# Channel mean and variance in a hybrid decoder layer: fp32 products replaced by high and low parts in the matmul's type

## The chip, the cores and the metric

The kernel runs on one core of a Trainium2 chip. The metric is device microseconds of one execution; lower is better. Engines: PE (TensorE, matmuls), DVE (VectorE), ACT (ScalarE), POOL (GpSimd) and SP (which issues most DMAs). Each takes its instructions from its own queue, in order.

## The reference

One decoder layer over 1024 tokens and 16 meta tokens, width 1024. What matters here is the convolution branch:

```python
c = c_val * jax.nn.sigmoid(c_gate)              # 512 channels
c = causal_dwconv(c, conv_dw, conv_dw_b)        # 31 taps
c = jax.nn.silu(layer_norm(c, conv_ln_g, conv_ln_b))
y_conv = c @ w_conv_proj

def layer_norm(x, g, b):
    xf = x.astype(jnp.float32)
    mu = xf.mean(-1, keepdims=True)
    var = jnp.square(xf - mu).mean(-1, keepdims=True)
    return ((xf - mu) * lax.rsqrt(var + LN_EPS) * g + b).astype(x.dtype)
```

The LayerNorm runs over the 512 channels of each token.

## The kernel before

Activations lie with channels on the partitions and tokens along the free axis. The convolution's result is four chunks of 128 channels, `acc[0..3]`, of U = 1026 tokens each. A sum over channels is therefore a sum over four tiles and then over 128 partitions; the second is a matmul with `ones`, a 128x128 tile that holds 1/512, which leaves the mean in every partition. `ones` and what it multiplies are fp32 (F); the kernel's other large products run in fp32r (R), each factor split into a high and a low part (`split`: a cast on ACT writes the high part, a subtraction on DVE the low one).

The tokens are handled in three groups, UG: 258, 384 and 384 columns. In order:

- `csum` (line 947) is the sum of the four chunks: two additions on POOL, one on DVE (L951).
- The means (L956): one matmul per group, `ones` times `csum`, into the PSUM tiles `ps_m`. Their rank is RK_EVAC, high; `after(ins, gate_mm[10][0])` keeps them behind the first part of gate tile 10.
- `cln_centre` (L998) subtracts the means on DVE, four operations per group.
- `cln_var` squares the four chunks on ACT (L1004, L1007), adds the squares on DVE (L1008) in temporaries of five buffers, and takes the sum over partitions with a matmul (L1010).
- `cln_rstd` takes a reciprocal root on ACT (L1015) and refines it by a Newton step on DVE (L1016 to L1019). `cln_scale` multiplies on DVE (L1026) and applies SiLU on ACT (L1027), all SiLUs behind the last root. `cln_split` writes the high and low parts of the result into `OC` (L1033, L1034) for the projection; `o_split` does the same for the attention's output.

The DVE operations from `cln_centre` to `o_split` are pinned: each is put behind the one before it (`pin`). The order of the calls is: centre of the groups 0, 1, 2; variance of 0, 1, 2; rstd 0, rstd 1, scale 0, rstd 2, scale 1, scale 2; then the splits.

At the same time PE multiplies the gate tiles (`gate_tile`, `z_group`): a tile is four groups of about 256 tokens, each 24 matmuls in fp32r (L339, L342, L343), into one of three accumulators with the tag "mm". ACT evacuates each with a Tanh (L735) and sends it to DRAM from its own queue (L128). The weights of each tile come by DMA and are split by ACT (L301) and DVE (L304). Behind the gate tiles the projections (`ps_p`) begin, which read `OA` and `OC`.

The order within a queue is fixed when the program is built: a planner takes the instruction of the best rank among those that it expects to be ready. Ranks that matter here: RK_SPLIT 500, RK_EVAC 600, RK_CLN 38000, RK_Z 40000; lower goes first. `after` adds an order between two instructions on one engine.

`ones` is made three times: at the start (it feeds the warm-up matmuls, L572), before the attention for the means, and after it for the variances.

Of the kernel before, what the change touches and what calls it, by code (L numbers as in the profile page):

```python
# [23 lines left out]
F = mybir.dt.float32  # L24
R = mybir.dt.float32r
AF = mybir.ActivationFunctionType
OP = mybir.AluOpType
AX = mybir.AxisListType

P = 128  # L30
# [6 lines left out]
U = T - U0  # L37
# [3 lines left out]
CW = 512  # L41
# [71 lines left out]
def tile_hybrid_layer(  # L113
# [3 lines left out]
    nc = tc.nc  # L117
    PSUM = bass.MemoryType.PSUM

    def dram(ap, offset, dims):  # L120
        return bass.AP(tensor=ap.tensor, offset=ap.offset + offset, ap=[list(d) for d in dims])

    def load(o, i):
        return nc.sync.dma_start(out=o, in_=i)
# [5 lines left out]
    def f32(ap):  # L130
        return ap.bitcast(F)

    def after(ins, first):

        tc.add_manual_dep(ins.ins, first.ins.name, mybir.DependencyInfo(
            mybir.DependencyClass.NoSync, mybir.DependencyReason.SCHED_ONLY), reason="order of work")

    @contextmanager
    def rank(p):

        saved = tc.cur_priority
        tc.cur_priority = p
        yield
        tc.cur_priority = saved
# [35 lines left out]
    start = ExitStack()  # L180
    sp = start.enter_context(tc.tile_pool(name="start", bufs=1, side="right", reuse_waits="tile"))
# [35 lines left out]
    cff, ident = (coll[:, a - n_right:b - n_right] for a, b in COLS[2:-1])  # L217
# [17 lines left out]
    b1col = lambda k: colA[:, 66 + k:67 + k]  # L235
    ffw = lambda t, c: cff[:, t * 44 + c:t * 44 + c + 1]

    def ones_of(pool, behind=None):
        t = pool.tile([P, P], F, name="ones", tag="ones", bufs=1)
        ins = nc.vector.memset(t, 1.0 / CW)  # L240
        if behind is not None:
            after(ins, behind)
        return t

    ones = ones_of(sp)
    qb = const2.tile([P, 4], F, name="qb")
    half_ = constr.tile([P, 1], F, name="half")
    nc.vector.memset(half_, 0.5)
# [70 lines left out]
    def weights(shape, fill):  # L319
        fills[0] += 1  # L320
        n = fills[0]
        own = n == 3
        raw = OB[:, 0:D].rearrange("p (k c) -> p k c", k=KC) if own else wraw(shape)
        with rank({1: 14, 2: 13, 3: 16, 4: 23}.get(n, RK_SPLIT)):
            last_fill.append(fill(raw))
        hi, lo = chunks(sp.tile([P, W_LEN], R, name="w3") if own else wsp())
        if n <= 3:
            return hi, lo, raw
        with rank(RK_SPLIT):
            last_split.append(split(raw, hi, lo))  # L330
            if n == 7:
                after(last_split[-1], cin_done[-1])
        return hi, lo
# [349 lines left out]
    ap = att.enter_context(tc.tile_pool(name="att", bufs=1, side="right", reuse_waits="tile"))  # L683
# [16 lines left out]
    def conv_chunk(c):  # L700
        sig = {}

        def g_evac(g, a, b, ps):
            sig[g] = stage(b - a)

            nc.scalar.activation(sig[g], ps, AF.Tanh, bias=bcol(10 + c), scale=0.5)  # L706
            nc.scalar.activation(sig[g], sig[g], AF.Identity, bias=half_, scale=0.5)

        gate_last.append(z_tile(in_cols(10 + c), ZG, g_evac, wt_c1 if c == 1 else None))
        cin = cp.tile([P, 16 + T], F, name="cin", tag="cin")  # L710
        nc.vector.memset(cin[:, 0:16], 0.0)

        def v_evac2(g, a, b, ps):
            cin_done.append(nc.vector.scalar_tensor_tensor(cin[:, 16 + a:16 + b], ps, bcol(6 + c), sig[g],
                                                           OP.add, OP.mult))

        z_tile(in_cols(6 + c), ZG, v_evac2)

        def taps():
            with rank(RK_CONV + c * 100):  # L720
                for j in range(TAPS):
                    wc = cdw[:, j * CH + c:j * CH + c + 1]
                    if j == 0:
                        nc.vector.tensor_scalar(acc[c], cin[:, j:j + U], wc, cdwb(c), OP.mult, OP.add)
                    else:
                        nc.vector.scalar_tensor_tensor(acc[c], cin[:, j:j + U], wc, acc[c], OP.mult, OP.add)  # L726

        return taps

    def gate_tile(i):  # L730
        b2, m = divmod(i, KC)

        def gate_evac(g, a, b, ps):
            t = stage(b - a)
            nc.scalar.activation(t, ps, AF.Tanh, bias=bcol(14 + i), scale=0.5)  # L735
            store(sgd[b2, m, :, a - U0:b - U0], t)

        gate_mm[i] = z_tile(in_cols(14 + i), TG, gate_evac)

    tc.cur_priority = RK_QKV + 2000  # L740
    ins = load(vd, dram(v1d, 0, [[0, P], [J_LEN, NH], [1, J_LEN]]))
# [11 lines left out]
    tc.cur_priority = RK_QKV + 5000  # L753
    cin8 = cin_done[-1]
    ones = ones_of(cp, cin8)
    vmT = ap.tile([P, 64], F, name="vmT")
    for t in (f32(vm[64:]), f32(pmTs[0][64:]), f32(pmTs[1][64:]), vmT):
        after(nc.vector.memset(t, 0.0), cin8)
    for g in range(NKV):
# [3 lines left out]
        for lo in (0, 64):  # L763
            for o, i in ((Kx[g][lo:, :, 16:144], kr[lo:, 16:T].rearrange("p (n c) -> p n c", c=P)),
                         (Kx[g][lo:, :, 0:16], kr[lo:, 0:16].unsqueeze(1).to_broadcast([P - lo, NB, 16]))):
                if lo == 0:
                    ins = nc.vector.tensor_copy(o, i)
                else:
                    ins = nc.vector.tensor_tensor(o, i, f32(o), OP.subtract)
# [11 lines left out]
    for q4 in range(2):  # L781
# [5 lines left out]
        for g in range(NKV):  # L787
            hi, lo = (V[:, q4 * 4:q4 * 4 + 4, g, i] for i in range(2))
# [22 lines left out]
    for h in range(NH):  # L811
        g, r = divmod(h, 4)
        o = ps[:2, h * 16:(h + 1) * 16]
        ins = nc.tensor.matmul(o, q0[g][0][:, r, 0:2], Kx[g][:, 0, 0:16], start=True, stop=False)
# [66 lines left out]
    for i in range(NB):  # L881
# [5 lines left out]
        for g in range(NKV):  # L887
            qh, ql = load_q(g, i) if i else (t[:, :, 2:] for t in q0[g])
            s = ap.tile([P, 4, 272], F, name="s", tag="s", bufs=3)
# [50 lines left out]
    for o in order:  # L940
        if isinstance(o, str):
            conv_chunk(int(o[1]))()
        else:
            gate_tile(o)
        if o == "c3":

            csum = cp.tile([P, 16 + T], F, name="csum", tag="cin")[:, :U]
            with rank(RK_EVAC):
                nc.gpsimd.tensor_tensor(csum, acc[0], acc[1], OP.add)
                nc.gpsimd.tensor_tensor(csum, csum, acc[2], OP.add)  # L950
                nc.vector.tensor_tensor(csum, csum, acc[3], OP.add)  # L951
    means = {}
    for g, (a, b) in enumerate(UG):
        with rank(RK_EVAC):
            means[g] = pat.tile([P, 512], F, name="ps_m", tag="st"[g % 2], bufs=2)
            ins = nc.tensor.matmul(means[g][:, :b - a], ones, csum[:, a:b], start=True, stop=True)  # L956
            after(ins, gate_mm[10][0])
    att.close()
    qsp_stack.close()

# [7 lines left out]
    tmp_p = tmp_stack.enter_context(tc.tile_pool(name="tmp", bufs=1, side="right", reuse_waits="tile"))  # L968

    ones = ones_of(tmp_p)  # L970

    def temp(n):
        return tmp_p.tile([P, 384], F, name="t", tag="t", bufs=5)[:, :n]

    def at_group(t, o, k, hl, a, b):

        x = k + hl * 4
        o += x * ZN - UG[0][1] if a else 8 * ZN + x * BS[0]
        return t[:, o + a:o + b]

    def conv(c, hl, a, b):
        return at_group(OC, OC_CV, c, hl, a, b)
# [3 lines left out]
    def pin(ins):  # L986

        if pinned:
            after(ins, pinned[-1])
        pinned.append(ins)  # L990

    dve = nc.vector
    sums, rstd, roots, silus = {}, {}, [], []
# [6 lines left out]
    def cln_var(g):  # L1000
        a, b = UG[g]
        n = b - a
        s_ = temp(n)
        nc.scalar.activation(s_, acc[0][:, a:b], AF.Square)  # L1004
        for c in range(1, CH):
            q_ = temp(n)
            nc.scalar.activation(q_, acc[c][:, a:b], AF.Square)  # L1007
            pin(dve.tensor_tensor(s_, s_, q_, OP.add))  # L1008
        sums[g] = pat.tile([P, 512], F, name="ps_m", tag="st"[g % 2], bufs=2)
        nc.tensor.matmul(sums[g][:, :n], ones, s_, start=True, stop=True)  # L1010

    def cln_rstd(g):
        n = UG[g][1] - UG[g][0]
# [42 lines left out]
    for g in range(3):  # L1056
        cln_var(g)
# [74 lines left out]
    for m in range(KC):  # L1132
        hi, lo = weights([P, KC, P], lambda raw: load(raw, w_ab[m]))
# [382 lines left out]
    for c in range(FC):  # L1516
        V4, X, Z, Y = (pup.tile([P, 1024], F, name=n, tag=n) for n in ("pw", "px", "pz", "py"))
        passes = ((1,), (0,)) if c == 0 else ((0, 1),)
        for subs in passes:
            last = subs == passes[-1]  # L1520
            w_next = iter(range(7))
            a, b = SUB[subs[0]][0], SUB[subs[-1]][1]
# [21 lines left out]
            def tt(*x):  # L1544
                with rank(RK_CHAIN):
                    return nc.vector.tensor_tensor(*x)  # L1546
# [30 lines left out]
            ins = tt(c22[:, a:b], c22[:, a:b], u13[:, a:b], OP.add)  # L1577
# [259 lines left out]
```

## Time and profile before

| | us |
|---|---|
| median of 3 runs | 1264.42 (1263.83 to 1264.93) |
| profiled execution | 1265.13 |
| its span | 1263.3 |
| means on PE (L956) | 349.5 to 351.25 of the span |
| variance sums on PE (L1010) | 358.9 to 365 |
| SiLUs on ACT (L1027) | 370.5 to 379.5 |
| first projection matmuls | from about 416 |

In the lines of the profile a time in front is microseconds from the start of the span, the next number the duration. `x6` counts instructions; an fp32 matmul shows as two. What stands in square brackets is idle time of the engine just before, and what ended it. In the list of waits the numbers are the total in us, how often, and the longest.

### The profile page before, as it was taken

How to read it: one execution, taken by the hardware profiler on the slowest of the kernel's cores; microseconds unless marked ns; L12 is line 12 of the kernel's file. 1: busy time of each engine (PE TensorE's matmuls, PEld its weight loads, DVE VectorE, ACT ScalarE, POOL GpSimd, SP SyncE). 2: the span in 40 equal slices, each digit the busy share in tenths (PEclk: the TensorE clock that was granted, in tenths of full speed). 3: DMA queues.
4: the chain of work that ended last, by engine and by line, in shares of the span. 5: the costliest groups of instructions: out<-in, count | busy, mean ns of one | idle time of the engine just before them, and what ended most of it. 6: DMA issues, size and time to landing. Idle time of an engine off the chain costs nothing.

```text
span 1263.3 us, 23034 instructions
## 1 busy us (share of the span) xinstructions
PE 1250.0 (99%) x9186; PEld 1182.3 (94%) x9186; DVE 1073.3 (85%) x1854; ACT 591.5 (47%) x1095; POOL 8.1 (1%) x9
## 2 busy tenths in 40 slices
PE   8999999999999999999999999999999999999997
PEld 8999999999999999788899999999999998888886
DVE  8888999999978577448999999998989977996697
ACT  7533355555472233335655555554555544444330
POOL 0000000001000000000000000000000000000000
PEclk9999999999999999999999999999999999999999
DMA  7385633432428354222145545454454566998712
GB/s 259 99 273 132 188 97 97 113 90 81 133 84 227 108 171 125 84 85 82 67 155 197 197 171 215 161 209 135 160 204 162 195 227 249 393 362 315 269 64 84
DMA packets 98701, 212.19 MB, mean 168 GB/s; under 512 B 11411, under 2 KB 38611, under 8 KB 98338
## 3 DMA queue, kind: packets, MB, share of 16 engines
q1 hardware_dynamic: 84474, 199.64, 47.3%
q10 hardware_dynamic: 14120, 11.08, 2.8%
q8 instruction: 72, 1.18, 0.4%
q14 instruction: 35, 0.29, 0.1%
HBM read 150.29 MB, written 62.70 MB: 169 GB/s over the span
## 4 chain that ended last, share of the span: by engine, by line
PE 93%; DVE 3%; DMA 2%; ACT 1%; issue 1%; SPq 0%; DVEq 0%; ACTq 0%
PE px L1538 14%; PE py L1538 9%; PE ps_x L1683 9%; PE ps_z L339 8%; PE ps_z L342 8%; PE ps_z L343 8%; PE ps_z L1683 5%; PE pz L1538 5%; PE pw L1538 5%; PE ps_p L342 2%; PE ps_p L339 2%; PE ps_p L343 2%; PE ps_w L343 2%; PE ps_w L339 2%; PE ps_w L342 2%; PE ps_z L557 2%
## 5 line engine op out<-in xcount | busy, mean ns | idle before, releaser
L339 PE MATMUL ps_z<-RHO,w 128*128 128x256 f32 (+2 forms) x864 | 243.9, 282 | 0.2 <-ACT FA L735 0.2
L342 PE MATMUL ps_z<-RHO,w 128*128 128x256 f32 (+2 forms) x864 | 243.6, 282 | 0.0
L343 PE MATMUL ps_z<-RHC,w 128*128 128x256 f32 (+2 forms) x864 | 243.1, 281 | 0.0
L339 PEld LDWEIGHTS ps_z<-RHO,w 128*128 128x128 f32 x864 | 162.8, 188 | 1.8 <-ACT FA L706 0.7
L342 PEld LDWEIGHTS ps_z<-RHO,w 128*128 128x128 f32 x864 | 162.5, 188 | 1.0
L343 PEld LDWEIGHTS ps_z<-RHC,w 128*128 128x128 f32 x864 | 162.7, 188 | 0.5
L726 DVE SCALAR_TENSOR_TENSOR FA<-cin,cdw,FA 128x1026 f32<-128x1026 f32 x120 | 152.4, 1280 | 0.7
L1360 DVE TENSOR_TENSOR RHO<-wr,RHO 128x512 fp32r<-128x512 f32 x94 | 64.0, 689 | 8.3 <-ACT RHO L1359 8.2
L1359 ACT CAST RHO<-wr 128x512 fp32r<-128x512 f32 x94 | 56.7, 619 | 23.3 <-DVE wr L1377 11.9
L301 ACT CAST w<-wr 128x1024 fp32r<-128x1024 f32 x37 | 38.8, 1048 | 60.4 <-PE ps_z L343 42.4
L735 ACT ACTIVATE FA<-ps_z,colr 128x258 f32<-128x258 f32 (+1 forms) x64 | 30.2, 473 | 69.5 <-PE ps_z L343 58.2
L1377 DVE TENSOR_TENSOR wr<-wr 128x512 f32<-128x512 f32 x88 | 60.6, 689 | 0.1
L304 DVE TENSOR_TENSOR w<-wr,w 128x1024 fp32r<-128x1024 f32 x37 | 45.1, 1219 | 17.9 <-ACT w L301 17.8
L1550 ACT COPY FA<-px 128x514 f32<-128x514 f32 (+2 forms) x23 | 13.2, 572 | 75.4 <-PE px L1538 75.4
L1360 DVE TENSOR_TENSOR w<-wr,w 128x512 fp32r<-128x512 f32 x60 | 40.8, 688 | 4.8 <-ACT w L1359 4.7
L1538 PE MATMUL px<-OA,RHO 128*128 128x258 f32 x324 | 43.2, 282 | 0.0
L1465 ACT ACTIVATE FA<-OB,coll 128x512 f32<-128x512 f32 x44 | 35.9, 815 | 14.9 <-DVE OB L1546 14.9
L1359 ACT CAST w<-wr 128x512 fp32r<-128x512 f32 x60 | 36.3, 618 | 13.9 <-DMA wr<-in_w_up_dram 6.8
L1538 PE MATMUL px<-OC,RHO 128*128 128x256 f32 x324 | 41.5, 277 | 0.0
L1550 ACT COPY OB<-px 128x514 f32<-128x514 f32 (+2 forms) x46 | 26.2, 569 | 32.7 <-PE px L1538 32.5
L1538 PE MATMUL px<-RHC,RHO 128*128 128x258 f32 (+1 forms) x312 | 41.1, 281 | 0.3 <-ACT OB L1550 0.3
L1538 PEld LDWEIGHTS px<-OA,RHO 128*128 128x128 f32 x324 | 40.5, 189 | 0.2 <-ACT OB L1550 0.2
(442 smaller groups left out, 3298.8 us busy)
## 6 DMA issues: line engine op xcount, KB each, us to landing
wr<-in_w_up_dram SPq DMA_DIRECT2D x44, 512.0 KB, 3.6
wr<-in_w_z_dram SPq DMA_DIRECT2D x29, 512.0 KB, 3.8
OB<-in_w_down_dram SPq DMA_DIRECT2D x24, 512.0 KB, 5.0
fd<-FA SPq DMA_DIRECT2D x44, 256.0 KB, 2.0
FA<-sd SPq DMA_DIRECT2D x15, 512.0 KB, 8.7
qt<-qd SPq DMA_DIRECT2D x28, 256.0 KB, 4.2
OB<-td SPq DMA_DIRECT2D x14, 512.0 KB, 9.9
sgd<-FA ACTq DMA_DIRECT2D x48, 128.0 KB, 2.9
```

Of the source, the lines that this page charges most:

```text
L301: ins = nc.scalar.copy(hi, raw)
L304: return nc.vector.tensor_tensor(lo, raw, f32(hi), OP.subtract)
L339: ins = nc.tensor.matmul(ps, al, bh, start=i == 0, stop=False)
L342: nc.tensor.matmul(ps, ah, bh, start=False, stop=False)
L343: last = nc.tensor.matmul(ps, ah, bl, start=False, stop=i == n - 1)
L726: nc.vector.scalar_tensor_tensor(acc[c], cin[:, j:j + U], wc, acc[c], OP.mult, OP.add)
L1359: nc.scalar.copy(hi, src)
L1360: ins = nc.vector.tensor_tensor(lo, src, f32(hi), OP.subtract)
L1377: ins = nc.vector.tensor_tensor(*x)
L1538: ins = nc.tensor.matmul(o, x[:, ks], bmat(sub, q, hl, k), start=first and k + j == 0, stop=k == 3 and j == 2, skip_group_check=not first)
L1550: copied.append(nc.scalar.copy(*x))
L1683: nc.tensor.matmul(banks[i], l[:, ts], r[:, ws], start=first and a and x + k == 0, stop=z and x == len(ops) - 1 and k == 2, skip_group_che ...
```

## The change

The means and the variance sums are taken as two fp32r products each. The thing to be summed is split into a high part, which ACT copies into fp32r, and a low part, which DVE subtracts; both are multiplied by `ones` in fp32r and accumulated in the same PSUM tile. 1/512 is a power of two. The parts of `csum` (`ch`, `cl`) are put into the buffers of the attention's scores (tag "s", three of them); those of the sum of squares (`hi`, `lo`) into the place in `OC` that `cln_split` fills for chunk 0 of the same group. The two later `ones` are made by a tensor_scalar operation on the identity matrix, in place of a memset.

```diff
-    def ones_of(pool, behind=None):
-        t = pool.tile([P, P], F, name="ones", tag="ones", bufs=1)
-        ins = nc.vector.memset(t, 1.0 / CW)
+    def ones_of(pool, behind=None, dtype=R):
+        t = pool.tile([P, P], dtype, name="ones", tag="ones", bufs=1)
+        if dtype is F:
+            ins = nc.vector.memset(t, 1.0 / CW)
+        else:
+            ins = nc.vector.tensor_scalar(t, ident, 0.0, 1.0 / CW, OP.mult, OP.add)
...
-    ones = ones_of(sp)
+    ones = ones_of(sp, dtype=F)
...
                 nc.vector.tensor_tensor(csum, csum, acc[3], OP.add)
+                ch, cl = (ap.tile([P, 4 * 272], R, name=n, tag="s", bufs=3)[:, :U] for n in ("ch", "cl"))
+                nc.scalar.copy(ch, csum)
+                nc.vector.tensor_tensor(cl, csum, f32(ch), OP.subtract)
...
-            ins = nc.tensor.matmul(means[g][:, :b - a], ones, csum[:, a:b], start=True, stop=True)
+            ins = nc.tensor.matmul(means[g][:, :b - a], ones, ch[:, a:b], start=True, stop=False)
             after(ins, gate_mm[10][0])
+            nc.tensor.matmul(means[g][:, :b - a], ones, cl[:, a:b], start=False, stop=True)
...
             pin(dve.tensor_tensor(s_, s_, q_, OP.add))
+        hi, lo = (conv(0, hl, a, b) for hl in range(2))
+        nc.scalar.copy(hi, s_)
+        pin(dve.tensor_tensor(lo, s_, f32(hi), OP.subtract))
         sums[g] = pat.tile([P, 512], F, name="ps_m", tag="st"[g % 2], bufs=2)
-        nc.tensor.matmul(sums[g][:, :n], ones, s_, start=True, stop=True)
+        nc.tensor.matmul(sums[g][:, :n], ones, hi, start=True, stop=False)
+        nc.tensor.matmul(sums[g][:, :n], ones, lo, start=False, stop=True)
```

## The prediction

> **What bounds the kernel now.** I read the page first, then the list of waits of the matmul engine (PE), then the chain of waits around the two places that change, and last the timelines of VectorE (DVE) and ScalarE (ACT) there.
>
> ```profile
> span 1263.3 us, 23034 instructions
> ...
> PE 1250.0 (99%) x9186; PEld 1182.3 (94%) x9186; DVE 1073.3 (85%) x1854; ACT 591.5 (47%) x1095; POOL 8.1 (1%) x9
> ```
>
> ```profile
> PE pw L1538 <- ACT FA L1340: 1.0, 1, 1.0
> PE ps_z L554 <- ACT FA L506: 0.3, 1, 0.3
> PE px L1538 <- ACT OB L1550: 0.3, 1, 0.3
> PE ps_z L1683 <- DVE RHC L1633: 0.2, 1, 0.2
> PE ps_z L1683 <- ACT RHC L1632: 0.2, 1, 0.2
> PE ps_z L339 <- ACT FA L735: 0.2, 1, 0.2
> ```
>
> PE works 99% of the span. After its start-up it waits hardly at all: the waits from 340 us on add up to 1.0 + 0.3 + 0.2 + 0.2 + 0.2 = 1.9 us. So a microsecond of PE work that goes is a microsecond gained, and work added to DVE or ACT costs only where it makes PE wait. The busy row of PE overstates it (pipelined matmuls overlap), so I price PE work by the spacing of starts, which the chain shows.
>
> **What is removed from PE.** The six fp32 matmuls with `ones` run as two passes each:
>
> ```profile
> 349.52 1.73 PE ps_m L956 x6
> ...
> 359.13 0.44 PE ps_m L1010 x2
> ...
> 361.23 0.66 PE ps_m L1010 x2
> ```
>
> The three means take 1.73 us. Of the variance sums the chain shows group 0 (258 columns, 0.44) and group 1 (384, 0.66); group 2 has the shape of group 1 and I give it 0.66. In all 1.73 + 0.44 + 0.66 + 0.66 = 3.49 us. The new ones are two matmuls each in the matmul's type (fp32r). Neighbours of that type give the price:
>
> ```profile
> 43.77 2.30 PE ps_z L557 x13
> ...
> 358.89 0.12 PE ps_z L343
> ```
>
> L557 has 384 columns here, 2.30/13 = 0.177 us each; the L343 of 358.89 has 258 columns, 0.12. So one set of three groups costs 2 x (0.12 + 0.177 + 0.177) = 0.95 us, both sets 1.90. PE's work falls by 3.49 - 1.90 = **1.59 us**. It cannot fall by more than 3.49 nor, since each pair replaces a pair of passes, would it rise unless an fp32r pass took longer than an fp32 one, which these rows exclude.
>
> **The copies for the means.** ACT writes `ch`, DVE writes `cl`, 1026 columns each, behind `csum` and ahead of the matmul.
>
> ```profile
> 345.26 1.23 DVE L951 TENSOR_TENSOR csum<-csum,FA 128x1026 f32<-128x1026 f32 x1
> 346.62 1.23 DVE L304 TENSOR_TENSOR w<-wr,w 128x1024 fp32r<-128x1024 f32 x1
> 349.99 5.14 DVE L998 TENSOR_TENSOR FA<-FA,ps_m 128x258 f32<-128x258 f32 x12 [2.15 <-PE ps_m L956]
> 355.05 3.86 DVE L1008 TENSOR_TENSOR t<-t 128x258 f32<-128x258 f32 x7
> 359.41 1.23 DVE L304 TENSOR_TENSOR w<-wr,w 128x1024 fp32r<-128x1024 f32 x1 [0.50 <-ACT w L301]
> ```
>
> The nearest rows are L304 for `cl` (1.23, a subtraction of 1024 columns into fp32r) and the cast L301 for `ch` (1.03, quoted below). `csum` is done at 346.49; ch can end near 348.0 (ACT starts a cast of weights and an evacuation in those two microseconds), cl behind L304 near 349.3. PE reaches L956 at 349.52, so even at its old place it waits between 0 and, if another 1.23 us of DVE gets in between, about 1.0 us. I take 0: DVE sits idle 2.15 us in front of L998, which is the cover. Without it the cost would be the whole 1.03 + 1.23 on the centring, still not on PE as long as PE has other tiles to multiply. The planner, which fixes each queue's order at build time by rank and expected readiness, will more likely put the matmuls some 2 us later on PE, among the same tiles; then centring is that much later. The tiles ch and cl lie in score buffers of the attention, which ended before 340 us. The two later `ones` become a tensor_scalar of 128 columns in place of a memset; at most a quarter of the 1.23 that L304 takes for 1024 columns, 0.3 us, and inside the same 2.15.
>
> **The copies for the variance.** Per group ACT gets a copy `hi` and DVE a subtraction `lo`; pinned DVE order puts lo(0) ahead of the adds of group 1, and lo(1) ahead of those of group 2. Behind hi on ACT stand evacuations of the z tiles; behind lo on DVE the adds, and for lo PE itself waits, since the sums matmul stands in its queue among the z matmuls.
>
> ```profile
> L1034 DVE TENSOR_TENSOR OC<-FA,OC 128x384 fp32r<-128x384 f32 x8 | 4.5, 558 | 0.3
> ```
>
> lo is 0.56 for 384 columns by L1034, the same subtraction, and about 0.43 for 258 (0.56 x 258/384 = 0.38 and a little for the start). For hi the square L1007 of 384 columns (0.51, below) is the nearest, so about 0.42, 0.51, 0.51. Added: DVE 1.55 us, ACT 1.44 us, with three handovers, so the chain from the centred values to the last variance sum grows by about 3 us. That delay by itself is covered: with the later means everything up to the last split comes about 5 us later, and DVE has
>
> ```profile
> 417.60 1.23 DVE L304 TENSOR_TENSOR w<-wr,w 128x1024 fp32r<-128x1024 f32 x1 [9.82 <-ACT w L301]
> ```
>
> 9.8 us idle before the projections begin to need it. What isn't covered is the order on ACT:
>
> ```profile
> 360.06 0.51 ACT L1007 ACTIVATE t<-FA 128x384 f32<-128x384 f32 x1
> 360.59 1.28 ACT L1015 ACT_TABLE_LOAD   x1
> 361.89 0.95 ACT L1015 ACTIVATE t<-ps_m,eps 128x258 f32<-128x258 f32 x2
> 362.85 1.28 ACT L735 ACT_TABLE_LOAD   x1
> 364.15 0.48 ACT L735 ACTIVATE FA<-ps_z,colr 128x258 f32<-128x258 f32 x1
> ...
> 365.07 1.28 ACT L1015 ACT_TABLE_LOAD   x1 [0.44 <-DVE t L1016]
> 366.36 0.58 ACT L1015 ACTIVATE t<-ps_m,eps 128x384 f32<-128x384 f32 x1
> 366.96 1.28 ACT L735 ACT_TABLE_LOAD   x1
> ...
> 374.54 1.03 ACT L301 CAST w<-wr 128x1024 fp32r<-128x1024 f32 x1
> ...
> 376.44 3.09 ACT L1027 ACTIVATE FA<-FA,colr 128x384 f32<-128x384 f32 x5
> 379.44 0.82 ACT L735 ACTIVATE FA<-ps_z,colr 128x258 f32<-128x258 f32 x2
> ```
>
> Today no ACT work stands between one group's root (L1015) and the next group's sum, and the roots of groups 0 and 1 share one table load, because their sums stand 361.23 - 359.13 = 2.1 us apart. With hi, lo and handovers they stand 2.1 + 0.5 + 0.6 + 0.1 = 3.3 us apart, more than one z tile (24 matmuls, about 2.8 us), so an evacuation with its own table falls between any two. And hi(1) is ready after root(0), so in ACT's queue it probably stands behind it. Then PE's sum(0) is followed by root(0): load 1.28, root 0.48; perhaps an evacuation: load 1.28, 0.48; then hi(1) 0.51, lo(1) 0.56, and some 0.4 of handovers and of sum(0) itself: 5.0 us with the evacuation, 3.2 without, against the 3.3 us of other matmuls that PE has between the two sums. So PE waits **1.7 us or nothing** at sum(1), and likewise at sum(2), where 1.23 us of a weight split (L304, today between groups 1 and 2) may widen the gap and leave 0.5. The evacuation falls between root and hi when it becomes ready in the 1.6 us between them, of every 2.8: a little over even, less the cases where it comes just ahead. I take two chances in five at each place, so one wait of the two is likeliest, and price it at 1.1, midway between 0.5 and 1.7, since both shapes of the gap stand in the rows above.
>
> [...]
>
> The other end of ACT's backlog today:
>
> ```profile
> 379.95 0.39 PE L339 MATMUL ps_z<-RHO,w 128*128 128x256 f32 x1 [0.15 <-ACT FA L735]
> ```
>
> Five SiLUs run ahead of an evacuation, and PE, with three accumulators, stands 0.15 us. In the new order DVE still has the Newton steps and the first scaling to do after the last root, which gives ACT time for its last table loads; I take this wait as gone (bounds: gone, or 2.56 more if another pair of loads lands behind the last root).
>
> **Sum.** The profiled execution took 1265.13 us, 1.83 around its span, 0.71 above the median of 1264.42 that I predict against. -1.59 (PE) - 0.15 (wait at 379.95) + 1.1 (one late sum) = -0.64, so 1264.49 for the profiled one and **1263.8** for the median.
>
> **The rivals.** (B) Both hi copies come ahead of the loads, or no evacuation falls in between: -1.59 - 0.15, 1262.7. For it: DVE's adds ran 2.5 us ahead of the sums today (first three done near 356.4, sum at 359.13). Against: root(0) waits for PE, which uses that lead up. (C) Slower: table loads get between PE's own sums. Both sums wait 1.7, and a further pair of loads, 2.56, lands on the evacuations, whose three accumulators are already used up at 379.95: -1.59 + 3.48 + 2.56 = +4.45, 1268.9. It decides from 4.1 us of PE waits on (1.59 + 2.53). For it: five loads in nine microseconds today, and ACT full there; against: PE must be unlucky three times. [...] (D) Faster beyond the matmuls: the queues after 400 us are laid out anew and the 1.0 + 0.3 + 0.2 + 0.2 of later waits go as well: 1264.42 - 1.59 - 0.15 - 1.7 = 1261.0. For it only that these waits exist. (E) The change doesn't do what it says: the pair of fp32r products costs what fp32 did and the copies come on top, at the likeliest wait: 1264.42 - 0.15 + 1.1 = 1265.4, against the rows of L557 and L343.
>
> **How the numbers follow.** Forecast 0.45, B 0.18, C 0.25, D 0.09, E 0.03. Of this kernel a difference under 0.2% (2.5 us) can't be told from none. Faster: D and about a quarter of B, which lies 1.7 below: 0.14. Slower: C and a little of the forecast's upper end: 0.27. The same: 0.59. The range reaches down to B with half of D's later waits, 1262.7 - 0.85 = 1261.8, and up to two full waits and one load, 1264.42 - 1.59 + 3.48 + 1.28 = 1267.6. The likeliest case alone lies between 1262.7 and 1264.4.
>
> **What would show it.** The six matmuls of each set should take 0.95 us in the chain, and the idle time before L998 should be filled by cl. The count of table loads between the first root and the first SiLU should rise from five to seven. PE should show a new wait of 0.5 to 1.7 us on lo at one of the sums, and the one on L735 near 380 should be gone. I am wrong if hi of group 1 stands ahead of root(0) on ACT (then B), if PE waits on sums or evacuations for more than 4 us (C), or if the difference arises after 420 us, where nothing here is changed.

## The result, and the profile after

Beside each other on the same chip, 20 runs each: before 1265.36 us median (1263.83 to 1266.35), after **1263.18 us** (1261.59 to 1265.29). The ratio is 0.9984, its 95% interval 0.9978 to 0.9990: 1.3 to 2.8 us less. The profiled execution after took 1263.24 us, its span is 1261.5.

The stage of the change is best measured between two matmuls whose work is the same in every version: the first of gate tile 10 (576 `ps_z` matmuls ahead of the projections) and the first projection `ps_p`. Rows of PE's timeline, before:

```profile
345.33 0.28 PE L339 MATMUL ps_z<-RHO,w 128*128 128x258 f32 x1
...
416.32 0.28 PE L339 MATMUL ps_p<-OA,w 128*128 128x258 f32 x1
```

and after:

```profile
346.88 0.28 PE L342 MATMUL ps_z<-RHO,w 128*128 128x258 f32 x1
...
415.49 0.28 PE L342 MATMUL ps_p<-OA,w 128*128 128x258 f32 x1
```

The stage took 70.99 us and takes 68.61, **2.38 less**. What lies ahead of it and behind it moves by some tenths of a microsecond in either direction between executions and doesn't belong to the change: the first z matmul starts between 55.0 and 57.3 us in the traces of this study. The new products, in the chain of waits after:

```profile
351.97 0.47 PE ps_m L962 x3
...
353.51 0.47 PE ps_m L964 x3
...
364.43 0.12 PE ps_m L1020
...
364.91 0.12 PE ps_m L1021
...
367.31 0.18 PE ps_m L1020
...
368.06 0.18 PE ps_m L1021
...
370.39 0.18 PE ps_m L1020
...
371.14 0.18 PE ps_m L1021
```

They add up to 1.90 us, where the fp32 passes took 3.49. PE's list of waits after:

```profile
PE ps_h L503 <- DVE xn L483: 2.0, 1, 2.0
PE ps_w L575 <- DVE ones L241: 1.1, 1, 1.1
PE pw L1549 <- ACT FA L1351: 1.0, 1, 1.0
PE ps_h L503 <- issue: 0.8, 1, 0.8
PE ps_s L899 <- DVE sm L903: 0.3, 1, 0.3
```

Neither a sum (L1020, L1021) nor an evacuation (L738, formerly L735) is in it: no new wait, and the one of 0.15 us at 379.95 has gone. The rest of the 2.38, that is 2.38 - 1.59 - 0.15 = 0.64, lies between the z matmuls. The view of stretches, for `ps_z` alone (stretch, length, busy time and count, granted clock, DMA), before:

```profile
364.00:395.00 31.00, 30.66 (x256) 1.00 0.51 136
```

and after:

```profile
364.00:395.00 31.00, 30.95 (x262) 1.00 0.37 113
```

Before, one variance sum (0.66) and the wait of 0.15 take their part, which leaves 30.19 us for 256 matmuls, 118 ns each; after, the three sums take 0.96, which leaves 30.04 us for 262, 115 ns each. The granted clock is 1.00 in both. Between the starts of two 256-column z matmuls this kernel has two usual distances, about 113 and about 118 ns, and it stays in one for many microseconds (its rhythm, below). Counted from 344 us on, 197 distances were of the long kind before and 68 after; 129 x 4.9 ns = 0.63 us.

That the two figures agree so closely is chance, for by the starts the wait cost more than the 0.15 of the list: the matmuls at 379.52, 379.95 and 380.18 stand 0.66 us apart in place of two distances of 118 ns, 0.42 more. After, 0.14 is lost in the same way at 387.7, where the list shows nothing. All other distances between z matmuls, scaled to the 576, add up to 0.54 less than before, and 1.59 + 0.28 + 0.54 = 2.41 is the better account of the 2.38.

ACT after, in its timeline from the first variance sum to the first SiLU:

```profile
364.08 0.51 ACT L1017 CAST OC<-t 128x384 fp32r<-128x384 f32 x1
...
365.68 1.28 ACT L1026 ACT_TABLE_LOAD   x1
...
366.98 0.48 ACT L1026 ACTIVATE t<-ps_m,eps 128x258 f32<-128x258 f32 x1
367.35 0.50 ACT L1017 CAST OC<-t 128x384 fp32r<-128x384 f32 x1
367.87 1.28 ACT L738 ACT_TABLE_LOAD   x1
...
369.66 1.28 ACT L1026 ACT_TABLE_LOAD   x1
...
372.49 1.28 ACT L738 ACT_TABLE_LOAD   x1
...
374.28 1.28 ACT L1026 ACT_TABLE_LOAD   x1
...
376.18 1.28 ACT L1038 ACT_TABLE_LOAD   x1
```

The hi copy of group 1 (364.08) stands ahead of the first root (366.98), that of group 2 (367.35) right behind it. There are six table loads, where there were five.

DVE around the means:

```profile
349.49 1.23 DVE L957 TENSOR_TENSOR cl<-csum,ch 128x1026 fp32r<-128x1026 f32 x1
353.66 2.82 DVE L1005 TENSOR_TENSOR FA<-FA,ps_m 128x258 f32<-128x258 f32 x7 [2.95 <-PE ps_m L964]
```

The means stand some 2.4 us later on PE, and DVE now idles 2.95 us ahead of the centring.

### The profile page after: what moved, and what is told of

Its sections match the earlier page's. It is cut to its first block, busy times and chain, and to the rows that moved or that the text cites. A ratio compares the mean times of both kernels' runs of the same rounds, so it can differ in the third digit from the quotient of the medians.

```text
span 1261.5 us, 23038 instructions
## 1 busy us (share of the span) xinstructions
PE 1247.8 (99%) x9186; PEld 1181.3 (94%) x9186; DVE 1076.5 (85%) x1858; ACT 595.0 (47%) x1100; POOL 8.0 (1%) x9
## 4 chain that ended last, share of the span: by engine, by line
PE 96%; DVE 2%; ACT 1%; DMA 0%; issue 0%; SPq 0%; DVEq 0%; ACTq 0%
PE px L1549 15%; PE py L1549 10%; PE ps_x L1694 9%; PE ps_z L342 8%; PE ps_z L345 8%; PE ps_z L346 8%; PE ps_z L1694 7%; PE pw L1549 5%; PE pz L1549 5%; PE ps_p L346 2%; PE ps_p L345 2%; PE ps_p L342 2%; PE ps_w L346 2%; PE ps_w L342 2%; PE ps_w L345 2%; PE ps_z L560 2%
## 5 line engine op out<-in xcount | busy, mean ns | idle before, releaser
L738 ACT ACTIVATE FA<-ps_z,colr 128x258 f32<-128x258 f32 (+1 forms) x64 | 30.1, 472 | 59.8 <-PE ps_z L346 48.9
```

## The experiments

Stage: from gate 10 to the first projection, read as above. Each ratio is to runs of the kernel before on the same chip.

| run | median us | ratio, 95% interval | stage us |
|---|---|---|---|
| before | 1265.36 | 1 | 70.99 |
| the change | 1263.18 | 0.9984 (0.9978 to 0.9990) | 68.61 |
| e1, means only | 1264.71 | 0.9993 (0.9984 to 1.0001) | 69.94 |
| e2, variances only | 1263.56 | 0.9987 (0.9978 to 0.9996) | 69.11 |
| e3, fp32 products twice | 1268.36 | 1.0020 (1.0011 to 1.0029) | 73.50 |
| e6, copies alone | 1263.95 | 0.9991 (0.9982 to 0.9999) | 69.89 |
| e4, hi behind the root | 1264.07 | 0.9993 (0.9983 to 1.0003) | 69.56 |
| e8, more table loads | 1284.52 | 1.0155 (1.0136 to 1.0173) | 77.81 |
| e5, high parts only | 1265.96 | 1.0011 (1.0002 to 1.0019) | 70.75 |
| e9, e5 and roots together | 1261.73 | 0.9975 (0.9964 to 0.9985) | 67.57 |
| e10, change and roots together | 1262.84 | 0.9983 (0.9974 to 0.9992) | 68.49 |
| e7, `ones` later | 1263.29 | 0.9986 (0.9977 to 0.9995) | 68.60 |
| e12, a small tile | 1276.48 | 1.0092 (1.0073 to 1.0110) | 69.99 |
| e13, a tile ahead of all | 1270.21 | 1.0042 (1.0022 to 1.0062) | 68.41 |

### What the products are worth, and what the rest is

**e1**: only the means are changed; the variance sums stay fp32.

```diff
-    ones = ones_of(tmp_p)
+    ones = ones_of(tmp_p, dtype=F)
...
-        nc.tensor.matmul(sums[g][:, :n], ones, hi, start=True, stop=False)
-        nc.tensor.matmul(sums[g][:, :n], ones, lo, start=False, stop=True)
+        nc.tensor.matmul(sums[g][:, :n], ones, s_, start=True, stop=True)
```

> Theory (the gain is the time of the passes on TensorE): only the three means run as two products in the matmul's type, so they take 0.95 us of TensorE in place of 1.73 and the stretch from the first z matmul of line 339 to the first projection falls from 360.9 us (before) by 0.8; in the time about 0.8 us less than before. Rival (the gain comes from another order of work in the queues, not from the products): 2.0 us less or no change, since the order is laid out anew here too. Rival (copies cost): VectorE's subtraction and ScalarE's copy ahead of the means would show as a wait of TensorE at the low part's product.

**e2**: the other half; the means stay fp32 and `ch`, `cl` aren't made.

```diff
-            ins = nc.tensor.matmul(means[g][:, :b - a], ones, ch[:, a:b], start=True, stop=False)
+            ins = nc.tensor.matmul(means[g][:, :b - a], ones, csum[:, a:b], start=True, stop=True)
```

> Theory: only the variance sums run as two products, 0.95 us of TensorE in place of about 1.76, so 0.8 us less than before, and with the 0.15 us wait at the evacuation gone perhaps 0.95. No wait of TensorE at the sums. Rival (order): 2.0 us less or no change. Rival (table loads between a high copy and its sum): TensorE waits 0.5 to 1.7 us at the sum of group 1 or 2 and the kernel is no faster than before.

**e3**: the kernel before with every fp32 product made twice, each with 1/1024.

```diff
-        ins = nc.vector.memset(t, 1.0 / CW)
+        ins = nc.vector.memset(t, 0.5 / CW)
...
-        nc.tensor.matmul(sums[g][:, :n], ones, s_, start=True, stop=True)
+        nc.tensor.matmul(sums[g][:, :n], ones, s_, start=True, stop=False)
+        nc.tensor.matmul(sums[g][:, :n], ones, s_, start=False, stop=True)
```

> The kernel before, with each fp32 product made twice with half the weight (1/1024) and accumulated; no copies. Theory: TensorE has 3.49 us more work in the same stage and nothing hides it, so the stretch to the first projection grows by 3.5 us to 364.4 and the time by about 3.5 us (0.28%). Rival (order): the time does not follow the work of TensorE, a change between -2 and +2 us.

**e6**: the change with all its copies made, but fp32 products of the unsplit sums; nobody reads the copies.

```diff
-            ins = nc.tensor.matmul(means[g][:, :b - a], ones, ch[:, a:b], start=True, stop=False)
+            ins = nc.tensor.matmul(means[g][:, :b - a], ones, csum[:, a:b], start=True, stop=True)
...
-        nc.tensor.matmul(sums[g][:, :n], ones, hi, start=True, stop=False)
-        nc.tensor.matmul(sums[g][:, :n], ones, lo, start=False, stop=True)
+        nc.tensor.matmul(sums[g][:, :n], ones, s_, start=True, stop=True)
```

> The copies and subtractions of the change are all made and kept in VectorE's and ScalarE's queues, but the products stay fp32, on the sums themselves. Theory: the copies lie beside TensorE's work, so the stretch to the first projection stays at 360.9 us within 0.3 and the time within 0.5 us of before. Rival (order): about 2 us less, since VectorE's and ScalarE's queues are laid out as in the change. Rival (copies cost): slower than before by up to 3 us, with TensorE waiting for the evacuations of line 735.

Doubling the products costs what their passes cost. In e3's chain:

```profile
350.59 1.73 PE ps_m L956 x6
352.32 1.73 PE ps_m L958 x6
...
364.50 0.65 PE ps_m L1011 x2
365.14 0.65 PE ps_m L1012 x2
```

The passes added are 1.73 + 0.43 + 0.65 + 0.65 = 3.46 us, and the stage grew by 2.51: here too the wait at 379.95 had gone, 0.42 us by the starts, and the long distances had fallen from 197 to 75 (0.60 us); 3.46 - 0.42 - 0.60 = 2.44. So the six products do stand wholly on the path that sets the end.

e6 is the surprise, outside what was expected of it. It removes nothing from PE and adds all the copies, and its stage is 1.10 us *shorter* than before; by its count of long distances (45) 0.74 of it is rhythm, and 0.42 is the wait. The copies cost nothing, as the cover on DVE and ACT let expect, and the shift to the faster rhythm doesn't need fp32r products. From e6 to the whole change the stage falls by another 1.28, near the 1.59 of PE's rows less 0.11 of rhythm and the 0.14 at 387.7. The two halves e1 (-1.05) and e2 (-1.88), of which about 0.8 and 0.8 to 0.95 were expected, add up to more than the whole (-2.38) for the same reason: e2 keeps only 16 long distances, e1 109. What sets the rhythm was not found; the versions, which differ in little but the order of this stage, each have their own count, and the stage moves by as much as 0.9 us (197 against 16 distances). The traces do show where it changes. In all versions but e8 and e12, where nearly every distance is long, each stretch of six or more long distances in this stage begins at most one z matmul behind a product with `ones`, of fp32 (before, 364.99; e6, 363.35) or of fp32r (the change, 352.28). Not every such product begins one, and e2 has no such stretch, so which of them do stays open. The 0.5 to 0.6 us of rhythm seem to go with where the products stand rather than with their passes, and another order could give them back.

### The wait that was forecast

**e4**: the order that the prediction had feared, by force: hi of group 1 behind root 0, hi of group 2 behind root 1. Three temporaries are left, and roots 0 and 1 have buffers of their own.

```diff
-        nc.scalar.copy(hi, s_)
+        cast = nc.scalar.copy(hi, s_)
+        if roots:
+            after(cast, roots[-1])
```

> The change, with the high copy of group 1 put behind the root of group 0 on ScalarE, and that of group 2 behind the root of group 1 (the order that the prediction took to be likely), the two roots in buffers of their own and three temporaries in place of five. By the prediction's arithmetic the chain from one sum to the next is 3.2 us (load 1.28, root 0.48, copy 0.51, subtraction 0.56, 0.4 of handovers) where no evacuation falls in between; the new order leaves some 33 matmuls, 3.9 us, between the sums, so TensorE should wait 0 to 0.3 us there. Rival (a table load in that chain always shows on TensorE): a wait of 1.3 us or more at one of the sums of groups 1 and 2.

No wait at the sums. PE's timeline in e4:

```profile
364.48 0.28 PE L1023 MATMUL ps_m<-OC,ones 128*128 128x258 f32 x1
...
368.23 0.34 PE L1022 MATMUL ps_m<-OC,ones 128*128 128x384 f32 x1
```

In the change these two starts are 367.31 - 364.91 = 2.40 us apart, here 3.75. The planner knows the longer chain (table load, root, hi, lo) and puts the next sum that much later among the z matmuls, as the order in PE's queue shows. PE goes on multiplying; only the sum comes later, and DVE has room for that. The stage is 0.95 longer than the change's: a wait of 0.3 at an evacuation (0.5 by the starts), and 184 long distances in place of 68, 0.57 us.

**e8**: e4, and three activations of one column between root and hi (Tanh, reciprocal root, Tanh), which put three more table loads there.

```diff
+            cln_root(g)
+            d_ = small.tile([P, 1], F, name="d_")
+            for f in (AF.Tanh, AF.Abs_reciprocal_sqrt, AF.Tanh):
+                ins = nc.scalar.activation(d_, eps, f)
+                after(ins, roots[-1])
+                roots.append(ins)
```

> As the run with the copies behind the roots, and between root and copy three operations of one column on ScalarE (Tanh, reciprocal root, Tanh), which bring three more table loads into the chain from one variance sum to the next: 7.7 us against the 38 and 45 matmuls (4.5 and 5.3 us) that the order leaves on TensorE between the sums. Theory (a table load counts as soon as it stands in the chain between two sums, because the order on TensorE makes no room for it): waits of about 3.2 and 2.4 us at the low parts of groups 1 and 2, and 4 to 6 us more in the time than the change. Rival (TensorE's work is so far behind VectorE's that the loads are covered): no wait over 0.5 us and no more than 1 us in the time.

Now the wait is there, 2.34 and 1.90 us at the two sums, somewhat below the sizes worked out; but the time rose by 19.6 us. PE's waits in the stage, e8:

```profile
PE ps_m L1022 <- ACT OC L1017: 4.2, 2, 2.3
```

Two things stand behind the rest. One is the granted clock. Stretches of one microsecond on PE, e8:

```profile
376.00:377.00 1.00, 0.31 (x2) 1.00 0.00 0
377.00:378.00 1.00, 1.00 (x8) 0.79 0.09 32
378.00:379.00 1.00, 1.00 (x7) 0.50 0.33 108
379.00:380.00 1.00, 1.00 (x6) 0.50 0.00 0
380.00:381.00 1.00, 1.00 (x7) 0.50 0.37 131
381.00:382.00 1.00, 1.00 (x10) 1.00 0.35 41
```

PE stood idle for 2.34 us up to 376.69; from about 377.6 to 381.0 the clock is 0.50, and the same follows the wait of 1.90 us at 386.5. From 377.86 to 380.87 the z matmuls start 0.215 us apart, from 381.06 on 0.118. Counted so, the work of 377.56 to 381.06 (one product of 384 columns and fifteen of 258) would have taken 1.95 us in place of 3.50, so the stretch cost 1.5 us, and the one behind the second wait (387.81 to 391.35, 0.213 us apart) cost 1.5 too. The first wait, 2.6 us by the starts, thus cost 4.1 in all. A wait of 2.14 us in e5 (below) left the clock at 1.00: it reads so from 378 to 386 us there, and the matmuls behind the wait, which ended at 378.77, start 0.114 us apart. The length of the gap alone doesn't set the three apart, and what does, these runs don't show.

The other thing is e8's second edit, the tile `d_`; e12 and e13 below show it.

### Fewer products, and slower

**e5**: the low parts are left out. DVE writes the sums in fp32r itself, and each group has one product; there are no copies. The sums are then held in fp32r alone, without a low part.

```diff
-            pin(dve.tensor_tensor(s_, s_, q_, OP.add))
-        hi, lo = (conv(0, hl, a, b) for hl in range(2))
-        nc.scalar.copy(hi, s_)
-        pin(dve.tensor_tensor(lo, s_, f32(hi), OP.subtract))
+            hi = conv(0, 0, a, b)
+            pin(dve.tensor_tensor(hi if c == CH - 1 else s_, s_, q_, OP.add))
...
-        nc.tensor.matmul(sums[g][:, :n], ones, hi, start=True, stop=False)
-        nc.tensor.matmul(sums[g][:, :n], ones, lo, start=False, stop=True)
+        nc.tensor.matmul(sums[g][:, :n], ones, hi, start=True, stop=True)
```

> The low parts are left out: VectorE writes the last addition of the channel sums, and of the sums of squares, straight into the matmul's type, and TensorE makes one product per group. No copies on ScalarE, no subtraction on VectorE. Theory: TensorE's work falls by another 0.95 us against the change (2.54 against before), so from the first matmul of gate tile 10 to the first projection 67.7 us in place of 68.6 (change) and 71.0 (before), give or take 0.6 for the spacing of TensorE's matmuls; in the time 1 us less than the change, 2.5 to 3.5 less than before. Rival (copies cost something after all): more than 1.6 us less than the change.

PE has 0.95 us less to do than in the change, 2.54 less than before, and by its time the kernel is slower than both, though its stage lies 0.24 us below that of before. What rival C said of the evacuations has come true here. PE's waits in the stage, e5:

```profile
PE ps_z L342 <- ACT FA L738: 2.6, 2, 2.1
```

and ACT's timeline:

```profile
361.87 1.28 ACT L1020 ACT_TABLE_LOAD   x1
...
363.66 1.28 ACT L738 ACT_TABLE_LOAD   x1
...
365.88 1.28 ACT L1020 ACT_TABLE_LOAD   x1 [0.44 <-ACT FA L738]
...
367.77 1.28 ACT L738 ACT_TABLE_LOAD   x1
...
369.93 1.28 ACT L1020 ACT_TABLE_LOAD   x1 [0.39 <-ACT FA L738]
...
371.82 1.28 ACT L738 ACT_TABLE_LOAD   x1
...
374.03 1.28 ACT L1032 ACT_TABLE_LOAD   x1 [0.44 <-DVE t L1024]
```

Every root has an evacuation between it and the next: seven loads, 9.0 us of ACT within 13.4, and the evacuations fall behind until PE has no free accumulator.

**e9**: e5 with the three roots side by side behind the last sum, so that they share one table load.

```diff
+    for g in (2, 0, 1):
+        cln_root(g)
     cln_rstd(0)
```

> As the run with the high parts alone, but with the three roots side by side on ACT, behind the last variance sum: roots 0 and 1 get buffers of their own, three temporaries are left, and one table load serves all three (3 loads in place of 7 up to the first SiLU). Theory (the 2.6 us that PE waited for evacuations there came from the pairs of table loads among them): the waits at L738 fall to 0.5 us or less, the stretch from gate 10 to the first projection from 70.75 to between 67.3 and 68.3 us, and the time lies 2.0 to 3.3 us below that run, 1.4 to 2.9 us below the kernel before. Rival (the waits come from the squares, which reach ACT in a shorter row once the copies are gone): the waits stay above 1.5 us and the stretch above 69.5.

ACT in e9:

```profile
366.44 1.28 ACT L1022 ACT_TABLE_LOAD   x1 [0.39 <-ACT FA L738]
367.73 0.58 ACT L1022 ACTIVATE t<-ps_m,eps 128x384 f32<-128x384 f32 x1
368.21 0.94 ACT L1022 ACTIVATE r<-ps_m,eps 128x258 f32<-128x258 f32 x2
...
370.10 1.28 ACT L738 ACT_TABLE_LOAD   x1
...
373.87 1.28 ACT L1041 ACT_TABLE_LOAD   x1 [1.12 <-DVE FA L1040]
```

Three loads in place of seven, no wait of PE in the stage, and the stage is 3.18 us shorter than e5's and 1.04 shorter than the change's, near the 0.95 that the missing products are worth. By the starts the two waits of e5 cost 0.73 and 2.41 us, 3.14 together. Against e5 the intervals lie apart (0.9964 to 0.9985 and 1.0002 to 1.0019); the gain on the median, 4.2 us, is a little more than the stage's. So the waits came from the loads. e9 is the fastest kernel of the study, by the stage; its interval overlaps that of the change.

**e10**: the change itself with the same three roots side by side.

> The change with the same three roots side by side on ACT (3 table loads in place of 6). Theory (in the change PE waits nowhere for ACT in this stretch, so loads saved there are worth nothing): waits of PE at the sums and evacuations stay at 0 to 0.3 us, the stretch from gate 10 to the first projection stays within 0.7 us of the change's 68.6, and the time within 0.1% of the change's. Rival (loads on ACT cost time by themselves, by their share of a full engine): three loads fewer, 3.8 us, show as at least 1.3 us in the stretch.

Three loads in place of six, and the stage changes by 0.12 us, the time not measurably. Where PE didn't wait for ACT, the table loads were free.

### What else could have moved the time

**e7**: where the means' product is fp32r, the attention's last products end some 5 us later against gate 10, and most of these traces show one more wait of 0.3 us (`ps_s`). This run makes the second `ones` behind `csum`, in case its earlier place on DVE is the cause.

```diff
-    ones = ones_of(cp, cin8)
...
+    with rank(RK_EVAC):
+        ones = ones_of(cp, cin8)
```

> The change, with the second ones tile made behind the channel sums in place of ahead of the attention. The change shows a wait of 0.3 us at a score matmul of the attention that the kernel before does not, and an order of work that differs there. Theory (the place of that one operation on VectorE sets off the other order in the attention): the wait goes and the last attention product comes near 336 us of the span, as before, in place of 342; the stretch from the first z matmul to gate tile 10 falls from 290.25 to 289.9 us, so 0.3 us in the time, too little to tell from none. Rival (the tiles for the copies set it off): the same as the change in all of these.

The wait stays, the stage is the change's within 0.01. The place of this operation isn't the cause; what is stays open. It is worth at most some 0.3 us.

**e12**: the change, and one unread tile of one column in the pool of small tiles. The pool keeps four buffers of each tile, so everything allocated behind it, the operands FA, RHC, RHO and OB among them, moves; the weights `w` lie ahead of it and stay. That the shift is 128 bytes per partition is my reckoning (the traces hold no addresses).

```diff
+    nc.gpsimd.memset(small.tile([P, 1], F, name="d_"), 0.0)
     dve = nc.vector
```

> The change and one more tile of one column in the pool of small tiles, which is set once by POOL and read by nobody; the order of all other work stays. The run with more table loads had such a tile too, and its 256-column matmuls stood 117.8 ns apart in place of 113.3 from 56 us on, long before the place of its edit. Theory (the tile moves the addresses of the buffers behind it, and PE reads the moved operands more slowly): the z tiles from 56 us on run at 117 to 118 ns, the stretch up to gate 10 takes some 294 us in place of 290.3, and the time is about 1279 us. Rival (that slow state belonged to that execution or to its ACT work): 113 to 114 ns, 290 us, and 1262 to 1264 us in all.

**e13**: the tile, 32 fp32 columns in one buffer (128 bytes per partition), is put ahead of the weights, so that both move alike.

```diff
-    nc.gpsimd.memset(small.tile([P, 1], F, name="d_"), 0.0)
+    nc.gpsimd.memset(const.tile([P, 32], F, name="d_"), 0.0)
```

(The lines with a minus are those of e12.)

> The change and one unread tile of 128 bytes per partition again, but ahead of the weight buffers too: weights (w) and the buffers of the moving operand (FA, RHC, RHO, OB) all move by 128 bytes, where in the run with the small tile only the latter moved by 128 and the weights stayed. Theory (what counts is how weights and moving operand lie to each other): the distance is that of the change again, so the z tiles run at 113 to 114 ns, the stretch up to gate 10 takes 290 us and the time is 1262 to 1264 us. Rival (what counts is the moving operand's own address): 117 to 118 ns, 294 us and about 1276 us as with the small tile.

One stretch far ahead of the change, full of z matmuls: PE in the change, with count and granted clock,

```profile
100.00:150.00 50.00, 50.00 (x448) 1.00 0.56 146
```

in e12,

```profile
100.00:150.00 50.00, 50.00 (x426) 1.00 0.54 136
```

and in e13:

```profile
100.00:150.00 50.00, 50.00 (x449) 1.00 0.59 153
```

With the tile PE gets through 5% fewer matmuls (426 in place of 448) at the same clock of 1.00, and with the weights moved too all are back (449). By stages (output: from the first `ps_w` behind the projections to the first `px`; up: from there to the down product; down: to PE's end):

| us | z to gate 10 | stage | output | up | down |
|---|---|---|---|---|---|
| the change | 290.25 | 68.61 | 104.66 | 436.44 | 209.88 |
| e12 | 294.00 | 69.99 | 106.02 | 439.79 | 213.23 |
| e13 | 289.93 | 68.41 | 105.20 | 440.15 | 213.23 |
| e8 | 294.03 | 77.81 | 106.02 | 439.87 | 213.23 |

For the z tiles e13's theory holds: moved alone, the operands took the stretch up to gate 10 from 290.25 us to 294.00, and with the weights moved as well it took 289.93. So here it counted how the weights lie to the moving operand, not where either lies. Its time (1270 us in place of 1262 to 1264) is missed, since I hadn't thought of the later stages: their operands also lie in buffers allocated from the other end of the memory (OC, RX), which didn't move in either run, so for them the distance has changed in both. The traces bear this out in the main; these are the mean distances in ns between the starts of like matmuls in a row, in the up and down products:

| operands | columns | one moved against the other in | the change | e12 | e13 |
|---|---|---|---|---|---|
| RHC, `w` (into `pw`) | 256 | e12 | 113.6 | 118.1 | 113.6 |
| OC, `w` (into `px`) | 256 | e13 | 114.6 | 114.4 | 118.0 |
| OC, RHO (into `py`) | 256 | both | 113.6 | 117.9 | 117.9 |
| RHC, RHO (into `pw`) | 256 | neither | 114.6 | 114.6 | 114.5 |
| OC, RHO (into `ps_x`) | 512 | both | 226.7 | 233.0 | 233.0 |

Smaller shifts, of 1 to 4 ns, show also in some products whose buffers kept their distance (RHC, RHO into `ps_x`, 512 columns: 226.7, then 230.6 in both), so this isn't the whole rule. (0.54 of the output stage in e13, whose operands OA, RHC and RHO all moved, stays unexplained.) e8 is thereby accounted for: its stages are e12's but for its own, 77.81 - 69.99 = 7.8, by the starts 4.8 of wait (4.2 in the list) and 3.1 of the clock at 0.50.

## Why the prediction was right, and where it wasn't

- **The number**: 1263.8 was forecast and 1263.18 measured, and that this is so near is partly luck. The drop was to be 0.64 us and was 2.18 on the medians; but the 20 runs of before have a median of 1265.36, 0.94 above the 1264.42 that the forecast started from, and this makes up for most of it.
- **PE's passes**: 3.49 us to 1.90, as worked out from L557 and L343, to the hundredth. e3 shows from the other side that these passes count in full. With that, rival E is out.
- **The wait at 379.95**: gone, as taken, but undersized: PE's work was priced by the spacing of starts and this wait by the list, 0.15 where the starts give 0.42. The bound above it, another pair of loads behind the last root, didn't occur.
- **The copies**: at nothing, rightly; e6 shows it. But of the means the idle time ahead of the centring wasn't "filled by cl", it grew from 2.15 to 2.95 us. The other sentence there holds: the planner put the means some 2.4 us later, and waiting moved with them.
- **The late sum, +1.1**: the step that failed. It said that "hi(1) is ready after root(0), so in ACT's queue it probably stands behind it", and priced one wait of PE. In the change hi(1) stands ahead of root(0), which the prediction itself had named as a sign of being wrong. And e4, with hi behind the root, has no wait either: the step had held the matmuls between two sums fixed at 3.3 us, but the planner lays out PE's queue anew with the chain it sees. e8 shows that the mechanism exists once the chain is made long enough, and that its price was too low, since in e8 the stretches at 0.50 add some 1.5 us to each of the two waits.
- **The loads**: six, not seven. e4 and e5 have the seven; e4 pays 0.3 us for it, e5 2.6.
- **The rhythm**: not in the prediction at all, worth 0.5 to 0.6 us. With the missing 1.1 it makes up most of the difference between the forecast of -0.64 and the stage's -2.38: 0.64 + 1.1 + 0.64 = 2.38, and of the last 0.64 some 0.1 is what the wait was undersized by.
- **The rivals**: what happened is B, by its own condition and nearly its time (-1.74 against -2.2 on the medians). C was a real danger: e5 shows it with less work on PE. D didn't occur: the wait of 1.0 at the up product is still there. (In C and in the range's upper end two waits of 1.7 are 3.4, not 3.48, which lowers both by 0.08 us.)

## What to carry to other kernels

Here PE was 99% busy, and passes on it counted with their full time (e3: 3.46 us added, of which the stage shows 2.51 and the wait and the rhythm that went account for 1.02), as long as the helpers' copies stayed ahead (e6: no cost). Look less at how much work goes to ACT and more at how often its tables change within one accumulator's turn, and put activations of one table side by side: from e5 to e9, with three loads of 1.28 us in place of seven, the stage fell by 3.18 us, while in e10, where PE had waited for none of them, three loads fewer moved it by 0.12. This planner, which knows the chain, placed the consumer behind it (e4: 3.75 us between two sums in place of 2.40, and no wait), so price a longer chain first at what the consumer's delay costs, and as a wait only where the queue can't be laid out anew (e8: 2.34 and 1.90 us). And before a slower variant is put down to its edit, look at a stretch far from it: one small tile moved the operands and cost 13.3 us of the span, more than any other single effect in this study.

## What was unexpected of the hardware

- How the buffers of a matmul's two operands lie to each other, moved here by one unread tile, made 113.6 or 118.1 ns per 256-column matmul (RHC, `w` into `pw`) and 226.7 or 233.0 per 512-column one (OC, RHO into `ps_x`), 13.3 us of the span (e12 against the change: 1274.8 and 1261.5). What it is in their places that costs the time, these runs don't show.
- The two distances, about 113 and 118 ns, also alternate within one kernel with the same buffers, in stretches of up to some tens of microseconds, worth up to 0.9 us in a stage of 70 (197 long ones before, 16 in e2). In this stage, e8 and e12 aside, each stretch of six or more long ones begins at most one z matmul behind a product with `ones`.
- Idle gaps of 2.34 and 1.90 us (e8) were each followed by some 3.4 us at a granted clock of 0.50; one of 2.14 us (e5) wasn't (1.00 behind it).
